# Strassen's algorithm for 10 of 44 block products in the last down projection of a two-layer encoder trunk

## The chip, the core and the metric

The kernel runs on one core of one Trainium2 chip. The metric is device time in microseconds (us). Three runs of the kernel before took 2696.85, 2698.23 and 2699.97 us; their median, 2698.23 us, is the time that counts.

## The reference

Two layers, each a token mixer (attention and a gating branch) and a gated convolutional FFN, and a last RMSNorm. The change touches the end of the second layer alone:

```python
def conv_ffn(h, w_up, conv_w, conv_b, w_down):
    ...
    return (jax.nn.gelu(acc) * b) @ w_down      # (256 x 5632) @ (5632 x 2048)

def reference(...):
    for l in range(DEPTH):                      # DEPTH = 2
        ...
        x = x + conv_ffn(rmsnorm(x, g_ffn[l]), w_up[l], conv_w[l], conv_b[l], w_down[l])
    return rmsnorm(x, g_final)
```

All tensors are float32; there are 256 rows (tokens) and 2048 columns of output.

## The kernel before

Every large product is float32 made of three products of the type float32r. `split_w` turns a tile of weights into two: ScalarE (ACT) copies it rounded, `hi` (line 109), and VectorE (DVE) subtracts, `lo = raw - hi` (line 110). The left operand is split likewise, once, into the two planes of an `operand()` tile. A product is then left_hi x hi + left_hi x lo + left_lo x hi: three matmuls of 512 columns (lines 118 to 120), which add up in one PSUM bank.

The last down projection takes the 22 tiles `gT[m]` as left operands. Each holds two k-tiles (`j` = 0, 1; 128 rows of the sum each) of 256 tokens in two halves (`t` = 0, 1). The output goes in four stretches `n` of 512 columns, one after the other. Within a stretch `rows()` walks `m` from 0 to 21: `fetch` brings 512 KB of weights (a tile `raw` of 128 x 2 x 512, issued by SyncE's queue, SP), `split_w` splits it, and TensorE (PE) does 2 `j` x 2 `t` x 3 = 12 matmuls. So a stretch is 264 matmuls and the projection 1056.

Buffers tie the engines together. There are five `raw` tiles: a fetch waits until an old tile has been split. There are three `hi` and three `lo` tiles: a split waits until PE has done with the tiles of the split three back, so that ACT and DVE run at most two splits ahead of the one PE works on. PSUM has eight banks: three pairs, `acc`, and two single ones, `tp`.

At the end of a stretch DVE adds the two banks to the residual (line 601), ACT sums squares (603) and GpSimd (POOL) multiplies by the gain `g_final` (605). The last stretch holds back the second half of the tokens for the last four `m` (`late=4`), so that the first half is done 24 matmuls before the second. Then for each half: the sum of squares is completed (612), POOL raises it to -1/2 (613), DVE and ACT scale the four stretches (618, 621), and they are written out.

Before the projection, POOL still makes the last two `gT` tiles (line 574, a product, and line 172, their second plane), and PE transposes the residual into `xb` through the `tp` banks (line 591; DVE copies out, 592).

The order in each engine's queue is set by a scheduler when the program is built; each queue is worked off strictly in that order. The functions that the change touches:

Of the kernel before, what the change touches and what calls it, by code (L numbers as in the profile page):

```python
# [41 lines left out]
def trunk_kernel(ctx, tc, x, g_mix, w_in, b_forget, g_sgu, w_spatial, b_spatial,  # L42
# [54 lines left out]
    def fetch(w2d, k0, nk, c0, cols):  # L97
        raw = wraw.tile([P, nk, cols], F32, tag="raw", name=nm("raw"))
        nc.sync.dma_start(raw, w2d[k0 * P:(k0 + nk) * P, c0:c0 + cols].rearrange("(k p) c -> p k c", p=P))
        return raw  # L100

    def split_w(raw, more=False, behind=None):
        shape = list(raw.shape)
# [5 lines left out]
        a = nc.scalar.copy(hi, raw)  # L109
        v = nc.vector.tensor_tensor(lo, raw, hi.bitcast(F32), op=ALU.subtract)  # L110
# [12 lines left out]
    def rows(w2d, c0, cols, ops, late=0):  # L123


        n = len(ops)
# [16 lines left out]
        return acc
# [443 lines left out]
    for m in range(KT // 2):
        tp = tp_bank()
        for k in range(2):
            for t in range(NT):  # L590
                nc.tensor.transpose(tp[:, (2 * t + k) * P:(2 * t + k + 1) * P], xT[m][:, k, t * P:(t + 1) * P], ident)
        nc.vector.tensor_copy(xb[m // 2][:, :, m % 2 * T:m % 2 * T + T], tp.rearrange("p (t c) -> p t c", t=NT))
    ss = small.tile([P, NT, NB], F32, tag="ss", name=nm("ss"))
    fin = small.tile([P, NT], F32, tag="fin", name=nm("fin"))
    for n in range(NB):
        gf = scratch([P, 512])
        nc.gpsimd.dma_start(gf, g_final[None, n * 512:(n + 1) * 512].broadcast_to([P, 512]))
        acc = rows(w_down[DEPTH - 1], n * 512, 512, gT, late=4 if n == NB - 1 else 0)
        for t in range(NT):
            z = xb[n][:, t, :]  # L600
            nc.vector.tensor_tensor(z, acc[t], z, op=ALU.add)
            junk = scratch([P, 512])
            nc.scalar.activation(junk, z, AF.Square, accum_out=ss[:, t, n:n + 1])
            if n < NB - 1:
                nc.gpsimd.tensor_tensor(z, z, gf, op=ALU.mult)
        if n == NB - 2:
            nc.vector.tensor_reduce(fin, ss[:, :, 0:NB - 1], axis=AX.X, op=ALU.add)
            nc.vector.tensor_scalar(fin, fin, 1.0 / D, EPS, op0=ALU.mult, op1=ALU.add)
    for t in range(NT):
        f_ = fin[:, t:t + 1]  # L610
        z = xb[NB - 1][:, t, :]
        nc.vector.scalar_tensor_tensor(f_, ss[:, t, NB - 1:NB], 1.0 / D, f_, op0=ALU.mult, op1=ALU.add)
        nc.gpsimd.tensor_tensor(f_, f_, mhalf[:, 0:1], op=ALU.pow)
        nc.vector.tensor_tensor(z, z, gf, op=ALU.mult)
        for n in range(NB):
            z = xb[n][:, t, :]
            if n % 2 == 0:
                nc.vector.tensor_scalar_mul(z, z, f_)
                nc.sync.dma_start(out_v[:, t, n * 512:(n + 1) * 512], z)
            else:  # L620
                nc.scalar.activation(z, z, AF.Identity, scale=f_)
# [30 lines left out]
```

## Time and profile before

| | |
|---|---|
| runs | 2696.85, 2698.23, 2699.97 us |
| profiled execution | 2697.62 us, of which span 2695.9 us |
| PE busy | 2681.0 us (99%) |
| DVE, ACT, POOL busy | 1608.7, 1268.8, 449.7 us |
| last projection | first matmul at 2444.74, last at 2686.59 us of the span |

A row of a timeline gives the start and the length in us, the engine, the line and operation, the tiles (out<-in), shapes, a count, and in brackets how long the engine idled before and what ended it. A PE row lasts longer than the step from one matmul to the next, because matmuls overlap in the array.

### The profile page before, as it was taken

Reading aid. Unit: us, or ns where it says so; the run is one execution under the profiler, and the core shown is the slowest. Engines: PE = TensorE matmul, PEld = TensorE weight load, DVE = VectorE, ACT = ScalarE, POOL = GpSimd, SP = SyncE. Lnnn points to the kernel's source line nnn. Section 1 sums busy time; section 2 is a strip of 40 time slices with the busy share of each in tenths; the row PEclk is TensorE's granted clock in tenths of the full one; section 3 lists DMA queues with packets and bytes.
Section 4 is the critical chain, followed back from the end, with each engine's and each line's share of the span. In section 5 each row is a group of like instructions: output and inputs, shape, how many; then the busy total and the mean of one; then the engine's idle time right before and its main releaser. Section 6 shows DMA issues by size and latency. Waiting matters only on the chain.

```text
span 2695.9 us, 36616 instructions
## 1 busy us (share of the span) xinstructions
PE 2681.0 (99%) x14384; PEld 2312.7 (86%) x14384; DVE 1608.7 (60%) x1728; ACT 1268.8 (47%) x1512; POOL 449.7 (17%) x381
## 2 busy tenths in 40 slices
PE   9999999999999999999999999999999999999998
PEld 7988888888888888888889888888888888888887
DVE  6555555566666676545555555555667676766444
ACT  5454554444444444444444545544544444444443
POOL 2201101112222222200002011011122222221000
PEclk9999999999999999999999999999999999999999
DMA  7566666656666666665665666666666666666664
GB/s 235 161 202 192 189 181 185 189 188 184 182 198 181 196 182 196 205 190 188 189 186 157 201 194 186 182 188 187 191 181 189 190 190 188 188 189 193 196 197 156
DMA packets 269557, 508.19 MB, mean 189 GB/s; under 512 B 16776, under 2 KB 33608, under 8 KB 269384
## 3 DMA queue, kind: packets, MB, share of 16 engines
q1 hardware_dynamic: 267144, 500.59, 61.5%
q0 software_dynamic: 1664, 4.21, 1.0%
q8 instruction: 112, 1.84, 0.3%
q10 hardware_dynamic: 576, 1.05, 0.1%
q14 instruction: 61, 0.50, 0.1%
HBM read 503.68 MB, written 2.11 MB: 188 GB/s over the span
## 4 chain that ended last, share of the span: by engine, by line
PE 97%; POOL 1%; issue 0%; ACT 0%; DMA 0%; DVE 0%; SPq 0%; POOLq 0%; ACTq 0%
PE acc L159 41%; PE acc L162 21%; PE acc L119 10%; PE acc L118 10%; PE acc L120 10%; PE tp L120 1%; PE tp L119 1%; PE tp L118 1%; POOL u L172 0%; POOL sq L190 0%; PE tp L522 0%; PE tp L467 0%; PE tp L484 0%; DMA u<-in_x_dram 0%; POOL tmp L418 0%
## 5 line engine op out<-in xcount | busy, mean ns | idle before, releaser
L110 DVE TENSOR_TENSOR lo<-raw,hi 128x1024 fp32r<-128x1024 f32 (+2 forms) x959 | 1221.9, 1278 | 1026.6 <-ACT hi L109 1025.5
L109 ACT CAST hi<-raw 128x1024 fp32r<-128x1024 f32 (+2 forms) x959 | 992.6, 1036 | 1223.9 <-PE acc L159 755.3
L159 PE MATMUL acc<-u,hi 128*128 128x512 f32 x4800 | 1485.7, 395 | 0.0
L162 PEld LDWEIGHTS acc<-u,lo 128*128 128x128 f32 x4800 | 883.2, 188 | 197.8 <-issue 0.9
L162 PE MATMUL acc<-u,lo 128*128 128x256 f32 x4800 | 927.7, 279 | 0.0
L159 PEld LDWEIGHTS acc<-u,hi 128*128 128x128 f32 x4800 | 744.6, 189 | 13.1
L119 PE MATMUL acc<-lo,u 128*128 128x512 f32 (+1 forms) x1352 | 521.1, 385 | 0.9 <-DVE lo L110 0.9
L118 PE MATMUL acc<-hi,u 128*128 128x512 f32 (+1 forms) x1352 | 517.6, 383 | 0.0
L120 PE MATMUL acc<-hi,u 128*128 128x512 f32 (+1 forms) x1352 | 515.3, 381 | 0.0
L119 PEld LDWEIGHTS acc<-lo,u 128*128 128x128 f32 x1352 | 254.8, 188 | 45.1 <-DVE lo L110 1.5
L118 PEld LDWEIGHTS acc<-hi,u 128*128 128x128 f32 x1352 | 254.7, 188 | 44.8
L120 PEld LDWEIGHTS acc<-hi,u 128*128 128x128 f32 x1352 | 254.6, 188 | 44.4
L558 POOL TENSOR_TENSOR tmp<-tmp,bc 128x512 f32<-128x512 f32 x44 | 58.3, 1325 | 373.5 <-DVE tmp L168 349.1
L565 DVE SCALAR_TENSOR_TENSOR tmp<-tmp,cv,tmp 128x256 f32<-128x256 f32 x176 | 117.5, 716 | 0.0
L190 POOL TENSOR_TENSOR sq<-sq,tmp 128x512 f32<-128x512 f32 x28 | 40.5, 1448 | 414.3 <-ACT tmp L189 413.2
L568 POOL TENSOR_TENSOR tmp<-tmp,bc 128x512 f32<-128x512 f32 x44 | 77.2, 1755 | 118.1 <-ACT tmp L567 118.1
L172 POOL TENSOR_TENSOR u<-tmp,u 128x512 fp32r<-128x512 f32 x52 | 88.2, 1701 | 32.4 <-ACT u L171 32.4
L574 POOL TENSOR_TENSOR tmp<-tmp,tmp 128x512 f32<-128x512 f32 x44 | 57.0, 1296 | 187.6 <-PE acc L162 152.1
L516 POOL TENSOR_TENSOR u<-u,tmp 128x512 f32<-128x512 f32 x16 | 28.3, 1789 | 319.0 <-DVE tmp L515 319.0
L167 ACT COPY tmp<-acc 128x512 f32<-128x512 f32 x112 | 65.2, 582 | 32.9 <-PE acc L162 32.9
L168 DVE TENSOR_TENSOR tmp<-acc,tmp 128x512 f32<-128x512 f32 x112 | 76.7, 685 | 1.2 <-ACT tmp L167 1.1
L567 ACT ACTIVATE tmp<-tmp 128x512 f32<-128x512 f32 x44 | 27.8, 631 | 53.4 <-DVE tmp L565 53.3
(159 smaller groups left out, 857.9 us busy)
## 6 DMA issues: line engine op xcount, KB each, us to landing
raw<-in_w_up_dram SPq DMA_DIRECT2D x352, 512.0 KB, 4.4
raw<-in_w_in_dram SPq DMA_DIRECT2D x255, 512.0 KB, 3.9
raw<-in_w_down_dram SPq DMA_DIRECT2D x176, 512.0 KB, 4.7
raw<-in_w_out_dram SPq DMA_DIRECT2D x64, 512.0 KB, 4.4
raw<-in_w_in_dram SPq DMA_DIRECT2D x48, 344.0 KB, 3.1
raw<-in_w_branch_b_dram SPq DMA_DIRECT2D x32, 512.0 KB, 4.5
raw<-in_w_branch_a_dram SPq DMA_DIRECT2D x32, 512.0 KB, 4.0
u<-in_x_dram SPq DMA_DIRECT2D x8, 256.0 KB, 7.0
```

Of the source, the lines that this page charges most:

```text
L109: a = nc.scalar.copy(hi, raw)
L110: v = nc.vector.tensor_tensor(lo, raw, hi.bitcast(F32), op=ALU.subtract)
L118: m0 = nc.tensor.matmul(o, lhsT=op[:, j, 0, ts], rhs=hi[:, jw, :], start=start, stop=False)
L119: nc.tensor.matmul(o, lhsT=op[:, j, 0, ts], rhs=lo[:, jw, :], start=False, stop=False)
L120: nc.tensor.matmul(o, lhsT=op[:, j, 1, ts], rhs=hi[:, jw, :], start=False, stop=stop)
L159: nc.tensor.matmul(acc[i][:, f, :], lhsT=hi[:, j, fs[f]], rhs=xhl, start=k == 0, stop=False, skip_group_check=True)
L162: nc.tensor.matmul(acc[i][:, f, 0:T], lhsT=lo[:, j, fs[f]], rhs=xh, start=False, stop=k == nk - 1, skip_group_check=True)
L167: nc.scalar.copy(dst, a[:, :, 1, :])
L168: nc.vector.tensor_tensor(dst, a[:, :, 0, :], dst, op=ALU.add)
L172: eng.tensor_tensor(op[:, :, 1, :], src, op[:, :, 0, :].bitcast(F32), op=ALU.subtract)
L565: nc.vector.scalar_tensor_tensor(y[:, f, :], a[:, f, tap:tap + T], cv[:, tap, ft:ft + 1], y[:, f, :], op0=ALU.mult, op1=ALU.add)
L568: nc.gpsimd.tensor_tensor(y, y, inv_b, op=ALU.mult)
```

## The change

The four stretches become two halves `g` of two stretches each (`q` = 0, 1), and each step `i` of a half brings two `raw` tiles, `ra` and `rb`, 1024 columns. For 17 of the 22 `m` nothing else changes: 24 matmuls ("a plain pair"). For five `m` (`AT`: steps 3, 7, 11, 15, 18 of half 0 and 1, 5, 9, 13, 17 of half 1) the 2 x 2 blocks of tokens and k-tiles times the 2 x 2 blocks of k-tiles and columns are multiplied by Strassen's algorithm in Winograd's form: seven products instead of eight, 21 matmuls. Each product or running sum has a bank of its own, eight in all: P1, P2, R3, Q4, R5, R6, R7, E.

The sums of weight blocks are done by DVE in float32, partly in place, and the four resulting sets are split. We call the splits of such a pair a (`ra`; products P1, P2), b (`rb` after line 680; R7, R3), c (`ra` after 684 and 685; R6, Q4) and d (`t1`, half size; R5). The sums of left blocks, `sums(m)`, are made once by POOL (one add over 512 columns, four subtracts of 128), copied by ACT (609), completed by DVE (610), and used by both halves. After the last such step of a half the banks P1, R5, R6, R7 are folded into the residual (lines 698 to 708). The last steps hold back two `m` instead of four.

```diff
+        nc.gpsimd.tensor_tensor(z, gT[m][:, :, 0, :].bitcast(F32), gT[m][:, :, 1, :].bitcast(F32), op=ALU.add)
+        nc.gpsimd.tensor_tensor(s_[:, 0, :], z[:, 0, P:T], z[:, 1, P:T], op=ALU.subtract)
...
+        nc.scalar.copy(hi, s_)
+        nc.vector.tensor_tensor(lo, s_, hi.bitcast(F32), op=ALU.subtract)
...
+    AT = ((3, 7, 11, 15, 18), (1, 5, 9, 13, 17))
+    LATE = 2
...
-    for n in range(NB):
-        acc = rows(w_down[DEPTH - 1], n * 512, 512, gT, late=4 if n == NB - 1 else 0)
+    for g in range(NB // 2):
+        b0, b1, b2, t0, t1_ = acc_banks(), acc_banks(), acc_banks(), tp_bank(), tp_bank()
+        bank = {"P2": b0[:, 0], "R3": b0[:, 1], "R6": b2[:, 0], "P1": b2[:, 1]}
+        bank.update({"Q4": b1[:, 0], "E": b1[:, 1], "R7": t0, "R5": t1_} if g == 0 else
+                    {"R7": b1[:, 0], "R5": b1[:, 1], "Q4": t0, "E": t1_})
...
+            nc.vector.tensor_tensor(t1, ra[:, 0, :], rb[:, 0, :], op=ALU.add)
+            nc.vector.tensor_tensor(rb[:, 0, :], rb[:, 0, :], rb[:, 1, :], op=ALU.add)
+            hi, lo = split_w(ra)
+            go("P1", A[0, 0], hi[:, 0, :], lo[:, 0, :], i == lastS)
+            go("P2", A[0, 1], hi[:, 1, :], lo[:, 1, :])
+            nc.vector.tensor_tensor(ra[:, 0, :], ra[:, 0, :], rb[:, 0, :], op=ALU.add)
+            nc.vector.tensor_tensor(ra[:, 1, :], ra[:, 1, :], ra[:, 0, :], op=ALU.add)
+            hi, lo = split_w(rb)
+            go("R7", s_[3], hi[:, 0, :], lo[:, 0, :], i == lastS)
+            go("R3", s_[4], hi[:, 1, :], lo[:, 1, :])
+            hi, lo = split_w(ra)
...
+            if i == lastS:
+                p1, v, z_ = scratch([P, 512]), scratch([P, 512]), scratch([P, 512])
+                nc.scalar.copy(p1, bank["P1"])
+                nc.vector.tensor_tensor(v, bank["R6"], p1, op=ALU.subtract)
...
+                nc.gpsimd.tensor_tensor(x[0, 0], x[0, 0], p1, op=ALU.add)
...
+                nc.gpsimd.tensor_tensor(x[1, 1], x[1, 1], z_, op=ALU.add)
```

Three places of the queues are of use below. First, POOL's queue at the start of the projection, before (`tmp` tiles are scratch, `u_20816` and `u_20823` the last two `gT`):

```order
L597 DMA tmp_20880<-in_g_final_dram 128x512
L574 TENSOR_TENSOR tmp_20812<-tmp_20812,tmp_20611 128x512
L574 TENSOR_TENSOR tmp_20819<-tmp_20819,tmp_20625 128x512
L172 TENSOR_TENSOR u_20816<-tmp_20812,u_20816 128x2x256
L172 TENSOR_TENSOR u_20823<-tmp_20819,u_20823 128x2x256
```

The same stretch of POOL's queue after:

```order
L604 TENSOR_TENSOR tmp_21007<-u_17241 128x512
L574 TENSOR_TENSOR tmp_20812<-tmp_20812,tmp_20611 128x512
L574 TENSOR_TENSOR tmp_20819<-tmp_20819,tmp_20625 128x512
L605 TENSOR_TENSOR tmp_21008<-tmp_21007 128x128
L607 TENSOR_TENSOR tmp_21008<-tmp_21007 128x128
L172 TENSOR_TENSOR u_20816<-tmp_20812,u_20816 128x2x256
L606 TENSOR_TENSOR tmp_21008<-tmp_21007,tmp_21008 128x128
L172 TENSOR_TENSOR u_20823<-tmp_20819,u_20823 128x2x256
L604 TENSOR_TENSOR tmp_21170<-u_18037 128x512
L608 TENSOR_TENSOR tmp_21008<-tmp_21007,tmp_21008 128x128
L605 TENSOR_TENSOR tmp_21171<-tmp_21170 128x128
```

The sums of left blocks for the first Strassen pairs are woven into the work that was there; those of the third, fourth and fifth pair follow at once. DVE's queue in the first Strassen pair, after (`lo_21032` is split b, `lo_21042` c, `lo_21052` d, `lo_21063` the next plain split; L594 copies a transposed tile out of a `tp` bank):

```order
L684 TENSOR_TENSOR raw_21003<-raw_21003,raw_21005 128x512
L685 TENSOR_TENSOR raw_21003<-raw_21003 128x512
L110 TENSOR_TENSOR lo_21032<-raw_21005,hi_21031 128x1024
L594 COPY u_20828<-tp_20854 128x2x256
L594 COPY u_20828<-tp_20860 128x2x256
L110 TENSOR_TENSOR lo_21042<-raw_21003,hi_21041 128x1024
L594 COPY u_20829<-tp_20866 128x2x256
L695 TENSOR_TENSOR lo_21052<-tmp_21016,hi_21051 128x512
L594 COPY u_20829<-tp_20872 128x2x256
L610 TENSOR_TENSOR u_20878<-tmp_21008,u_20878 128x512
L610 TENSOR_TENSOR u_20879<-tmp_21171,u_20879 128x512
L110 TENSOR_TENSOR lo_21063<-raw_21058,hi_21062 128x1024
```

The copies that free the `tp` banks stand between the splits; banks R7 and R5 of half 0 are these `tp` banks. Second, DVE's queue where one stretch ended and the next began, before:

```order
L110 TENSOR_TENSOR lo_22128<-raw_22125,hi_22127 128x1024
L601 TENSOR_TENSOR u_20828<-acc_21696,u_20828 128x512 x2
L110 TENSOR_TENSOR lo_22146<-raw_22143,hi_22145 128x1024
L607 TENSOR_REDUCE fin_20879<-ss_20878 128x2
L608 TENSOR_SCALAR fin_20879<-fin_20879 128x2
L110 TENSOR_TENSOR lo_22164<-raw_22161,hi_22163 128x1024
```

After, at the seam of the two halves (`lo_21830` is the last split of half 1's plain step 0, `lo_21865` split a and `lo_21877` split b of its Strassen step 1):

```order
L110 TENSOR_TENSOR lo_21830<-raw_21823,hi_21829 128x1024
L716 TENSOR_TENSOR u_20826<-acc_20890,u_20826 128x512
L716 TENSOR_TENSOR u_20827<-acc_20890,u_20827 128x512
L716 TENSOR_TENSOR u_20826<-acc_20891,u_20826 128x512
L716 TENSOR_TENSOR u_20827<-acc_20891,u_20827 128x512
L110 TENSOR_TENSOR lo_21865<-raw_21857,hi_21864 128x1024
L679 TENSOR_TENSOR tmp_21861<-raw_21857,raw_21859 128x512
L722 TENSOR_REDUCE fin_20885<-ss_20884 128x2
L680 TENSOR_TENSOR raw_21859<-raw_21859 128x512
L723 TENSOR_SCALAR fin_20885<-fin_20885 128x2
L684 TENSOR_TENSOR raw_21857<-raw_21857,raw_21859 128x512
L685 TENSOR_TENSOR raw_21857<-raw_21857 128x512
```

Four evictions stand where two stood, and a Strassen pair's sums right behind them. Third, the end of DVE's queue, before:

```order
L601 TENSOR_TENSOR u_20829<-tp_22105,u_20829 128x512
L612 SCALAR_TENSOR_TENSOR fin_20879<-ss_20878,fin_20879 128x1
L614 TENSOR_TENSOR u_20829<-u_20829,tmp_22103 128x512
L618 TENSOR_SCALAR u_20826<-u_20826,fin_20879 128x512
L618 TENSOR_SCALAR u_20828<-u_20828,fin_20879 128x512
L601 TENSOR_TENSOR u_20829<-tp_22106,u_20829 128x512
L612 SCALAR_TENSOR_TENSOR fin_20879<-ss_20878,fin_20879 128x1
```

And after (`tp_21819` is bank Q4, `tp_21820` bank E, which PE fills last):

```order
L716 TENSOR_TENSOR u_20828<-tp_21819,u_20828 128x512
L727 SCALAR_TENSOR_TENSOR fin_20885<-ss_20884,fin_20885 128x1
L731 TENSOR_TENSOR u_20828<-u_20828,tmp_21812 128x512
L727 SCALAR_TENSOR_TENSOR fin_20885<-ss_20884,fin_20885 128x1
L731 TENSOR_TENSOR u_20829<-u_20829,tmp_21813 128x512
L727 SCALAR_TENSOR_TENSOR fin_20885<-ss_20884,fin_20885 128x1
L731 TENSOR_TENSOR u_20828<-u_20828,tmp_21812 128x512
L735 TENSOR_SCALAR u_20826<-u_20826,fin_20885 128x512
L735 TENSOR_SCALAR u_20828<-u_20828,fin_20885 128x512
L716 TENSOR_TENSOR u_20829<-tp_21820,u_20829 128x512
L727 SCALAR_TENSOR_TENSOR fin_20885<-ss_20884,fin_20885 128x1
```

Between the eviction of Q4 and that of E now stand eight operations of DVE, where four stood between the last two evictions before. PE's order keeps `hi` before `lo` in a plain step: two matmuls with the new `hi`, then one with the new `lo`.

More of the change, by code (lines that the diff above doesn't have):

```diff
@@ new lines, in trunk_kernel, with three @@
+    NG = FT // 2
+    AT = ((3, 7, 11, 15, 18), (1, 5, 9, 13, 17))
+    LATE = 2
+    S = []
+    for i in range(len(AT[0])):
+        if i < 4:
+            u_ = unit([2, 4, P], F32R)
+            hi, lo = u_[:, 0], u_[:, 1]
+        else:
+            hi, lo = (xpool.tile([P, 4, P], F32R, tag=f"x{2 * (i - 4) + q}", name=nm("sx")) for q in range(2))
+        S.append((hi, lo))
+    Sx = {}
+    def three(bank, started, A, hi, lo, last):
+        for q, (l_, r_) in enumerate(((A[0], hi), (A[0], lo), (A[1], hi))):
+            nc.tensor.matmul(bank, lhsT=l_, rhs=r_, start=q == 0 and not started, stop=last and q == 2)
@@ L593, in trunk_kernel, with go, plain @@
     ss = small.tile([P, NT, NB], F32, tag="ss", name=nm("ss"))
     fin = small.tile([P, NT], F32, tag="fin", name=nm("fin"))
-    for n in range(NB):
-        gf = scratch([P, 512])
-        nc.gpsimd.dma_start(gf, g_final[None, n * 512:(n + 1) * 512].broadcast_to([P, 512]))
-        acc = rows(w_down[DEPTH - 1], n * 512, 512, gT, late=4 if n == NB - 1 else 0)
-        for t in range(NT):
[L600 to L607, printed above, removed]
+    for g in range(NB // 2):
+        n0 = 2 * g
+        gf = [scratch([P, 512]) for _ in range(2)]
+        for q in range(2):
+            nc.gpsimd.dma_start(gf[q], g_final[None, (n0 + q) * 512:(n0 + q + 1) * 512].broadcast_to([P, 512]))
+        b0, b1, b2, t0, t1_ = acc_banks(), acc_banks(), acc_banks(), tp_bank(), tp_bank()
+        bank = {"P2": b0[:, 0], "R3": b0[:, 1], "R6": b2[:, 0], "P1": b2[:, 1]}
+        bank.update({"Q4": b1[:, 0], "E": b1[:, 1], "R7": t0, "R5": t1_} if g == 0 else
+                    {"R7": b1[:, 0], "R5": b1[:, 1], "Q4": t0, "E": t1_})
+        seen = set()
+        order = list(range(NG))
+        paired = dict(zip(AT[g], AT[0]))
+        if g == 1:
+            rest = [m for m in range(NG) if m not in AT[0]]
+            order = []
+            for i in range(NG):
+                order.append(paired[i] if i in paired else rest.pop(0))
+        w2d = w_down[DEPTH - 1]
+        held = []
+        def go(name, A, hi, lo, last=False):
+            three(bank[name], name in seen, A, hi, lo, last)
+            seen.add(name)
+        out_of = {(0, 0): "P2", (0, 1): "R3", (1, 0): "Q4", (1, 1): "E"}
+        def plain(A, ws, t, last):
+            for q in range(2):
+                for j in range(2):
+                    go(out_of[t, q], A[t, j], ws[q][0][:, j, :], ws[q][1][:, j, :], last and j == 1)
+        lastS = max(paired)
+        for i, m in enumerate(order):
+            A = left(m)
+            ra, rb = (fetch(w2d, 2 * m, 2, (n0 + q) * 512, 512) for q in range(2))
+            if i not in paired:
+                late = g == 1 and NG - i <= LATE
+                ws = [split_w(r_, more=late and i < NG - 1) for r_ in (ra, rb)]
+                if late:
+                    held.append((A, ws, i == NG - 1))
+                for t in range(1 if late else NT):
+                    plain(A, ws, t, i == NG - 1)
+                continue
+            if m not in Sx:
+                Sx[m] = sums(m, *S[AT[0].index(m)])
+            s_ = Sx[m]
+            t1 = scratch([P, 512])
+            nc.vector.tensor_tensor(t1, ra[:, 0, :], rb[:, 0, :], op=ALU.add)
[9 more added lines that the diff above has]
+            hi, lo = split_w(ra)
+            go("R6", s_[2], hi[:, 0, :], lo[:, 0, :], i == lastS)
+            go("Q4", A[1, 1], hi[:, 1, :], lo[:, 1, :])
+            hi = wspl.tile([P, 512], F32R, tag="hi", name=nm("hi"))
+            lo = wspl.tile([P, 512], F32R, tag="lo", name=nm("lo"))
+            nc.scalar.copy(hi, t1)
+            nc.vector.tensor_tensor(lo, t1, hi.bitcast(F32), op=ALU.subtract)
+            go("R5", s_[1], hi, lo, i == lastS)
+            if i == lastS:
+                p1, v, z_ = scratch([P, 512]), scratch([P, 512]), scratch([P, 512])
+                nc.scalar.copy(p1, bank["P1"])
+                nc.vector.tensor_tensor(v, bank["R6"], p1, op=ALU.subtract)
+                nc.vector.tensor_tensor(z_, bank["R7"], v, op=ALU.add)
+                x = {(t, q): xb[n0 + q][:, t, :] for t in range(NT) for q in range(2)}
+                nc.gpsimd.tensor_tensor(x[0, 0], x[0, 0], p1, op=ALU.add)
+                nc.vector.tensor_tensor(x[0, 1], bank["R5"], x[0, 1], op=ALU.add)
+                nc.vector.tensor_tensor(x[1, 1], bank["R5"], x[1, 1], op=ALU.add)
+                nc.gpsimd.tensor_tensor(x[0, 1], x[0, 1], v, op=ALU.add)
+                nc.gpsimd.tensor_tensor(x[1, 0], x[1, 0], z_, op=ALU.subtract)
+                nc.gpsimd.tensor_tensor(x[1, 1], x[1, 1], z_, op=ALU.add)
+        for q in range(2):
+            for A, ws, last in held:
+                for j in range(2):
+                    go(out_of[1, q], A[1, j], ws[q][0][:, j, :], ws[q][1][:, j, :], last and j == 1)
+        for t in range(NT):
+            for q in range(2):
+                z = x[t, q]
+                nc.vector.tensor_tensor(z, bank[out_of[t, q]], z, op=ALU.add)
+                junk = scratch([P, 512])
+                nc.scalar.activation(junk, z, AF.Square, accum_out=ss[:, t, n0 + q:n0 + q + 1])
+                if g == 0:
+                    nc.gpsimd.tensor_tensor(z, z, gf[q], op=ALU.mult)
+        if g == 0:
+            nc.vector.tensor_reduce(fin, ss[:, :, 0:2], axis=AX.X, op=ALU.add)
```

17 lines of the change are left out of this document (14 added, 3 removed).

## The prediction

> **What bounds the kernel now.** I read the page's busy times and its chain first, then a window of the last projection.
>
> ```profile
> PE 2681.0 (99%) x14384; PEld 2312.7 (86%) x14384; DVE 1608.7 (60%) x1728; ACT 1268.8 (47%) x1512; POOL 449.7 (17%) x381
> PE 97%; POOL 1%; issue 0%; ACT 0%; DMA 0%; DVE 0%; SPq 0%; POOLq 0%; ACTq 0%
> 2500.00:2560.00 60.00, 60.00 (x266) 49.70 (x266) 28.99 (x24) 24.60 (x27) 3.59 (x3) 1.00 0.64 198
> ```
>
> PE is the bound, in the whole and in this stage; the window's columns after the length are PE, PE's weight loads, DVE, ACT, POOL, clock, DMA share, GB/s. So a matmul taken away is time won, if everything that feeds PE keeps its lead. The timeline shows that lead:
>
> ```profile
> 2512.52 0.39 PE L120 MATMUL acc<-hi,u 128*128 128x512 f32 x1
> 2512.74 0.39 PE L118 MATMUL acc<-hi,u 128*128 128x512 f32 x1
> 2512.99 1.05 ACT L109 CAST hi<-raw 128x1024 fp32r<-128x1024 f32 x1 [1.67 <-PE acc L120]
> 2514.07 1.22 DVE L110 TENSOR_TENSOR lo<-raw,hi 128x1024 fp32r<-128x1024 f32 x1 [0.66 <-ACT hi L109]
> 2515.24 0.39 PE L120 MATMUL acc<-hi,u 128*128 128x512 f32 x1
> ```
>
> Twelve matmuls start in 2515.24 - 2512.52 = 2.72 us, 0.227 us each. When a split's last matmul is through, ACT refills its buffer 0.25 us after the next split's first matmul; `lo` ends at 2515.29, 2.55 us after that matmul. PE has two more splits ready, 5.44 us, so 2.9 us are spare.
>
> **What DVE and POOL do to each other.** Duration alone doesn't tell what the added sums cost:
>
> ```profile
> 2508.71 1.22 DVE L110 TENSOR_TENSOR lo<-raw,hi 128x1024 fp32r<-128x1024 f32 x1
> 2509.27 3.06 POOL L605 TENSOR_TENSOR u<-u,tmp 128x512 f32<-128x512 f32 x2 [54.77 <-ACT tmp L603]
> 2511.35 2.06 DVE L110 TENSOR_TENSOR lo<-raw,hi 128x1024 fp32r<-128x1024 f32 x1 [1.43 <-ACT hi L109]
> 2628.95 3.05 POOL L605 TENSOR_TENSOR u<-u,tmp 128x512 f32<-128x512 f32 x2 [56.26 <-ACT tmp L603]
> 2629.71 1.07 DVE L608 TENSOR_SCALAR fin<-fin 128x2 f32<-128x2 f32 x1
> 2449.38 4.59 POOL L172 TENSOR_TENSOR u<-tmp,u 128x512 fp32r<-128x512 f32 x2
> 2450.42 1.27 DVE L592 COPY u<-tp 128x512 f32<-128x512 f32 x2
> ```
>
> A DVE split that starts inside a POOL operation ends 1.08 us after it (2511.35 + 2.06 = 2513.41, POOL's end 2512.33): it stood still and then ran its 1.22, less 0.14 of overlap. Even a 128x2 operation took 1.07. The split at 2508.71, which was first, lost nothing, and POOL's two took 3.06. Copies out of PSUM beside POOL ran at 0.64 each, undisturbed. So POOL's and DVE's operations on SBUF exclude each other, first come first served. The Trainium skill, "SBUF — State Buffer", section "Who interferes with whom", states this as an exclusive lock for the whole instruction, taken by a tensor_tensor with both inputs in SBUF against GpSimd's reads, and not by one with an input in PSUM; by that rule the sum is the one below, and were they independent it would be that of the second rival. The trace agrees (2.06 against 1.22). Durations for what is added:
>
> ```profile
> L574 POOL TENSOR_TENSOR tmp<-tmp,tmp 128x512 f32<-128x512 f32 x44 | 57.0, 1296 | 187.6 <-PE acc L162 152.1 <-DVE tmp L168 35.5
> L198 POOL TENSOR_TENSOR sq<-sq 128x256 f32<-128x256 f32 x4 | 4.0, 998 | 0.3
> L614 DVE TENSOR_TENSOR u<-u,tmp 128x512 f32<-128x512 f32 x2 | 1.4, 688 | 0.0
> L601 DVE TENSOR_TENSOR u<-acc,u 128x512 f32<-128x512 f32 x6 | 3.9, 686 | 1.2 <-PE acc L120 1.2
> L171 ACT CAST u<-tmp 128x512 fp32r<-128x512 f32 x52 | 32.0, 619 | 8.3 <-POOL tmp L418 5.4 <-POOL tmp L574 0.9
> raw<-in_w_down_dram SPq DMA_DIRECT2D x82, 512.0 KB, 4.7
> 2466.91 0.87 PE tp L591 x8
> 2444.74 0.40 PE L118 MATMUL acc<-hi,u 128*128 128x512 f32 x1
> 2445.79 1.59 DVE L110 TENSOR_TENSOR lo<-raw,hi 128x1024 fp32r<-128x1024 f32 x1 [0.93 <-ACT hi L109]
> ```
>
> POOL's 128-column subtract isn't in the trace: between a quarter of L574 (0.32) and half of L198 (0.50); I take 0.46, nearer the row of smaller size, since a fixed part doesn't shrink. On SBUF a POOL operation then blocks DVE for its length less 0.14: 1.15 and 0.32.
>
> **The sum, term by term.**
>
> *Matmuls gone:* 10 pairs x 3 x 0.227 = -6.8 us. SP still issues the same 88 fetches of 512 KB; ACT gets 10 casts for split d and 5 for the sums (0.62 each, 25 of 60 us busy): no cost.
>
> *Eight steady pairs.* DVE does 4 x 0.69 + 3 x 1.22 + 0.69 = 7.1 us in such a pair against PE's 21 x 0.227 = 4.8; with three plain pairs 14.4 against 21.1. On average it fits, so what counts is the lead. Splits a, b, c feed six matmuls each (1.36 us), d three. The next plain split takes b's buffer: from b's last matmul it needs 0.25 + 1.05 + 0.03 + 1.22 + 0.05 = 2.6 us to its `lo`; PE has nine matmuls of c and d and two with the new `hi`: 2.5. It waits 0.1, and about as much once more before the lead is back: 8 x 0.15 = +1.2. Ends: 0, and 0.5 a pair (4) where a late sum or fetch adds to it.
>
> *The first pair* (half 0, step 3). PE would reach its fifth batch of transposes in this stage 19.4 us after the stage's first matmul (72 + 6 matmuls, 16 transposes at 0.11). They need a `tp` bank that DVE's copy frees, and that copy stands behind split b. From 1.05 us on (the row at 2445.79) DVE has six splits and four sums on SBUF before it, 10.1 us. POOL, which has its two products, two second planes and the sums for the coming pairs, gets between them six operations of 512 columns and some eight small ones: 6 x 1.15 + 8 x 0.32 = 9.5. Together 20.7, the copy 0.6: PE waits 1.7. Behind it bank R5 waits for the last copy, after c and d (0.8), and the third matmul of R7 for the sums' second plane (0.4). Now b is released late, near the pair's end: the next plain `hi` comes 0.9 after PE is free, and its `lo`, behind another POOL operation, 1.3 later. Sum +5.2. Ends: 1.7 (only the last two, without POOL) and 6.5 (small operations of 0.6).
>
> *The seam* (half 1, step 1). Count from half 0's last matmul. DVE's four evictions end at 2.6. POOL's four gain multiplies ask from 2.2 on, each as soon as a square is summed, and one gets in ahead of each of DVE's next long operations: split a ends at 4.6, the first sum at 6.3, the sum for b at 8.1, the 128x2 step at 9.3, the two sums for c at 10.7. PE has a plain pair (5.4) and a (1.4), so it wants b's `hi` at 6.8 and gets it at 9.2; two matmuls on it wants c's at 9.7 and gets it at 11.8; the second plain `hi`, needed early in PE's order, costs 0.4. +5.0. Ends: 1.2 without POOL, 6. Before, a stretch's end had two evictions, each followed by plain splits with 2.9 us spare.
>
> *The two folds.* After each half's last Strassen step DVE has the difference and the two evictions of R5 (2.1 us) between the first and the second plain split, which would be done 0.5 us late, and one POOL add in front of it: 2 x 1.0 = +2.0; ends 1 and 3.
>
> *The end.*
>
> ```profile
> 2686.59 0.39 PE L120 MATMUL tp<-hi,u 128*128 128x512 f32 x1
> 2687.02 0.69 DVE L601 TENSOR_TENSOR u<-tp,u 128x512 f32<-128x512 f32 x1 [1.84 <-PE tp L120]
> 2687.75 0.63 ACT L603 ACTIVATE tmp<-u 128x512 f32<-128x512 f32 x1 [2.11 <-DVE u L601]
> 2688.50 0.16 DVE L612 SCALAR_TENSOR_TENSOR fin<-ss,fin 128x1 f32<-128x1 f32 x1 [0.79 <-ACT tmp L603]
> 2688.74 0.94 POOL L613 TENSOR_TENSOR fin<-fin,mhalf 128x1 f32<-128x1 f32 x1 [4.47 <-DVE fin L612]
> 2689.72 1.33 ACT L621 ACTIVATE u<-u,fin 128x512 f32<-128x512 f32 x2 [1.25 <-POOL fin L613]
> 2684.30 0.88 DVE L618 TENSOR_SCALAR u<-u,fin 128x512 f32<-128x512 f32 x2 [0.47 <-POOL fin L613]
> ```
>
> The last eviction now starts 0.43 us after the last matmul starts, and all else follows. After the change Q4 ends twelve matmuls earlier, so its eviction starts at -2.72 + 0.43 = -2.29, and between it and E's stand three operations of 0.16, three of 0.69 and two of 0.44: with itself 4.1 us. E's eviction starts at 1.8 instead of 0.43. The chain behind it is the same: +1.4; ends 1.2 and 2.2 (POOL's power blocking DVE).
>
> Sum: -6.8 + 1.2 + 5.2 + 5.0 + 2.0 + 1.4 = +8.0 us. The profiled execution took 2697.62 us, 0.6 under the median of the runs shown; on the median that gives 2706.2.
>
> **Rivals.**
>
> *The lead covers all.* If the waits at the first pair, the seam, the folds and the steady pairs don't come, because splits run further ahead than I step them, the matmuls' 6.8 us come in but for the end's 1.4: 2692.8. About 0.2%, 5.4 us, is what a measurement here tells from no change, so this ends faster only if all added waits, the end's with them, stay under 1.4. For it: DVE idles half of the window. Against it: the lead is two splits, and at the three places DVE owes more than that.
>
> *POOL falls into DVE's gaps.* Without exclusion the first pair costs 2.5, the seam 1.2, the folds 1.1, with 1.2 and 1.4 as above: 7.4 - 6.8 = +0.6, 2698.8. For it: 94% of the window has no POOL work. Against it: POOL's work is set free by the very evictions and stage start that load DVE.
>
> *Fetches stop DVE.* The first sum of a pair, t1, needs the weights of both stretches and stands in DVE's queue ahead of a plain split. By the five buffers, b's fetch goes out when the split five before it is done, some 2.1 us before PE starts on that one; it lands at +2.6, t1 takes 0.7 and the plain split 1.2: 4.5, against 5.4 when PE wants it. Landings of 6.5 us would cost 1 us in each of ten pairs: 10 more than forecast, 2716. Against it:
>
> ```profile
> SPq L99 <- DVE lo L110: 183.2, 80, 3.2
> ```
>
> SP's queue waited 183 us for freed buffers in this stage; it isn't behind.
>
> That the change does not do what it says is excluded: PE's queue has 30 matmuls less.
>
> **How the numbers follow.** My forecast, exclusion at the three places: 0.64. POOL in the gaps: 0.22. Fetches: 0.09. The lead covers all: 0.05. Likeliest 2706.2; its own range, from half of the waits at the three places (12.2 / 2 = 6.1 less) to 5 us more, 2700 to 2711. The range reaches down past the second rival, to 2697.5, and up to 2712; outside lie the first rival and most of the fetches. Faster by over 0.2%: 0.05. Within 0.2% (2692.8 to 2703.6): 0.22 and, of the forecast's lower end, 0.08, together 0.30. Slower: 0.65.
>
> **What will show it.** Right: PE idles in the waits view on DVE `lo` and ACT `hi` at the first pair (about 20 to 29 us into the stage) and 7 to 13 us after half 1 begins, under 0.3 us in the pairs between; DVE splits of about 2 us there, beside POOL. The stage's matmuls span some 248 to 249 us, not 242, and the last matmul to the span's end 1.4 us more than now (9.3). Wrong: PE idle under 3 us in the stage, or DVE's splits at 1.22 beside POOL; or idle at every pair, released by a DMA.

## The result, and the profile after

The changed kernel takes 2710.62 us (median of 4 runs, 2708.36 to 2712.35), the one before 2698.20 (4 runs): ratio 1.0045, 95% interval 1.0033 to 1.0057. It is slower by more than the 0.2% that can be told apart. The forecast was 2706.2, its range 2697.5 to 2712.0. The profiled execution took 2711.51 us with a span of 2709.8, so 13.9 us more than the profiled one before. The page's busy times and the head of its chain:

```profile
PE 2683.8 (99%) x14354; PEld 2307.7 (85%) x14354; DVE 1670.6 (62%) x1805; ACT 1287.8 (48%) x1539; POOL 485.0 (18%) x412
PE 95%; DVE 2%; POOL 1%; DMA 1%; issue 1%; ACT 1%; SPq 0%; POOLq 0%; DVEq 0%; ACTq 0%
```

PE has its 30 matmuls less, and yet 2.8 us more busy time: some matmuls got longer. DVE, 0% of the chain before, is 2% now. The same 60 us of the last projection that the prediction showed for the kernel before:

```profile
2500.00:2560.00 60.00, 59.36 (x260) 48.05 (x259) 42.48 (x46) 30.31 (x32) 3.74 (x5) 1.00 0.62 194
```

DVE went from 29.0 to 42.5 us in it and PE stood idle for only 0.6: in the middle of a half the pairs cost little. So most of the loss is at a few places. The waits of the last projection (who waited for whom, total, times, longest):

```profile
DVE tmp L679 <- DMA raw<-in_w_down_dram: 27.4, 9, 4.8
...
PE acc L628 <- ACT hi L109: 4.7, 3, 3.4
PE acc L628 <- DVE lo L110: 4.0, 5, 1.4
...
PE tp L593 <- DVE u L594: 1.2, 1, 1.2
```

*The first pair.* PE's waits there come where the forecast had them: 1.3 us on the copy of a transposed tile, 0.5 on the one that frees bank R5, 0.8 on the next plain `hi`, 1.6 on its `lo`. Beside POOL, DVE's operations stretch (timeline; start, duration; in brackets the idle time before and its releaser):

```profile
2461.82 1.61 POOL L604 TENSOR_TENSOR tmp<-u 128x512 f32<-128x512 f32 x1
2462.33 1.66 DVE L685 TENSOR_TENSOR raw<-raw 128x512 f32<-128x512 f32 x1
2471.53 1.28 POOL L604 TENSOR_TENSOR tmp<-u 128x512 f32<-128x512 f32 x1
2471.76 3.54 DVE L110 TENSOR_TENSOR lo<-raw,hi 128x1024 fp32r<-128x1024 f32 x2 [1.03 <-ACT hi L109]
2473.95 0.50 PE L628 MATMUL acc<-lo,u 128*128 128x512 f32 x1 [1.44 <-DVE lo L110]
```

The weight sum for c takes 1.66 us where 0.69 is free, two splits 3.54 where 2.4 are, and PE stands behind them.

*The seam.* DVE, POOL, ACT and PE after half 0's last matmul:

```profile
2572.35 2.48 DVE L716 TENSOR_TENSOR u<-acc,u 128x512 f32<-128x512 f32 x4
2574.59 1.30 POOL L720 TENSOR_TENSOR u<-u,tmp 128x512 f32<-128x512 f32 x1 [10.17 <-ACT tmp L718]
2574.75 2.23 DVE L110 TENSOR_TENSOR lo<-raw,hi 128x1024 fp32r<-128x1024 f32 x1
2576.44 1.70 POOL L720 TENSOR_TENSOR u<-u,tmp 128x512 f32<-128x512 f32 x1
2576.90 1.78 DVE L679 TENSOR_TENSOR tmp<-raw,raw 128x512 f32<-128x512 f32 x1
2578.67 2.51 POOL L720 TENSOR_TENSOR u<-u,tmp 128x512 f32<-128x512 f32 x2
2578.71 3.02 DVE L680 TENSOR_TENSOR raw<-raw 128x512 f32<-128x512 f32 x1
2581.90 1.04 ACT L109 CAST hi<-raw 128x1024 fp32r<-128x1024 f32 x1 [5.54 <-DVE fin L723]
2583.00 0.73 PE L628 MATMUL acc<-hi,u 128*128 128x512 f32 x2 [3.40 <-ACT hi L109]
```

Split a and the two sums behind it take 2.23, 1.78 and 3.02 where 1.22, 0.69 and 0.69 are free: 4.4 us, which is the seam's wait. The sum for b waits out two gain multiplies in one go. (The cast at 2581.90 waits for that sum's end at 2581.73; the view names the 128x2 step that ended just after it.)

*What the forecast had no term for.* The windows view, cut where the granted clock changes (columns: length, PE, PEld, DVE, ACT, POOL, clock, DMA share, GB/s):

```profile
2471.05:2474.46 3.41, 1.30 (x5) 0.77 (x5) 2.70 (x2) 2.57 (x3) 3.26 (x4) 1.00 0.03 10
2474.46:2477.88 3.42, 3.42 (x9) 2.66 (x9) 2.23 (x2) 0.00 (x0) 3.00 (x3) 0.50 0.65 196
...
2580.28:2583.69 3.41, 0.69 (x2) 0.30 (x2) 3.38 (x5) 1.44 (x2) 0.90 (x1) 1.00 0.08 25
2583.69:2587.10 3.41, 2.75 (x7) 2.17 (x7) 2.46 (x3) 1.18 (x2) 0.00 (x0) 0.50 0.36 112
2587.10:2590.52 3.42, 3.42 (x9) 2.67 (x8) 1.23 (x1) 2.07 (x3) 0.00 (x0) 0.50 0.64 200
```

After each of the two places PE ran at half its clock, one stretch of 3.41 us and one of 6.83, with 9 matmuls in a full window where 15 fit. That is +4.5 us.

*A sum that waits for a transfer,* at the pairs at steps 9 and 17 of half 1:

```profile
2615.65 1.23 DVE L110 TENSOR_TENSOR lo<-raw,hi 128x1024 fp32r<-128x1024 f32 x1 [1.04 <-ACT hi L109]
2617.51 1.05 ACT L109 CAST hi<-raw 128x1024 fp32r<-128x1024 f32 x1 [1.89 <-PE tp L628]
2621.67 0.69 DVE L679 TENSOR_TENSOR tmp<-raw,raw 128x512 f32<-128x512 f32 x1 [4.79 <-DMA raw<-in_w_down_dram]
2624.27 0.50 PE L628 MATMUL acc<-lo,u 128*128 128x512 f32 x1 [1.14 <-DVE lo L110]
...
2665.23 0.69 DVE L679 TENSOR_TENSOR tmp<-raw,raw 128x512 f32<-128x512 f32 x1 [4.09 <-DMA raw<-in_w_down_dram]
2667.84 0.50 PE L628 MATMUL acc<-lo,u 128*128 128x512 f32 x1 [0.43 <-DVE lo L110]
```

The cast of the plain split before the pair at step 9 was done at 2618.56, but its `lo` stood behind `t1` in DVE's queue, and `t1` waited until 2621.67 for b's weights. PE lost 1.4 us around it, and 0.7 in the same way ahead of step 17.

*The end.* The last matmul starts at 2699.56:

```profile
2700.01 0.88 DVE L735 TENSOR_SCALAR u<-u,fin 128x512 f32<-128x512 f32 x2
2700.81 0.68 DVE L716 TENSOR_TENSOR u<-tp,u 128x512 f32<-128x512 f32 x1
```

Bank E's eviction starts 1.25 us after it (0.43 before), behind the scalings of the first 128 tokens.

The account of the two profiled executions, from the starts of successive matmuls (a matmul is worth 0.2267 us, a transpose 0.109, what is over is lost):

| term | forecast | measured |
|---|---|---|
| matmuls gone | -6.8 | -6.8 |
| first pair | +5.2 | +5.0 |
| seam | +5.0 | +4.5 |
| two folds | +2.0 | +0.9 (half 0's; half 1's cost nothing) |
| eight steady pairs | +1.2 | +4.7 (1.4 and 0.7 of it ahead of steps 9 and 17 of half 1) |
| the end | +1.4 | +0.9 |
| half clock behind first pair and seam | none | +4.5 (1.6 and 3.0) |
| before the stage | none | +0.2 |
| sum | +8.0 | +13.9 |

The two folds differ in DVE's queue:

```profile
2556.17 0.68 DVE L704 TENSOR_TENSOR u<-tp,u 128x512 f32<-128x512 f32 x1
2556.76 0.68 DVE L705 TENSOR_TENSOR u<-tp,u 128x512 f32<-128x512 f32 x1
2557.36 1.94 DVE L110 TENSOR_TENSOR lo<-raw,hi 128x1024 fp32r<-128x1024 f32 x1
...
2678.12 0.68 DVE L700 TENSOR_TENSOR tmp<-acc,tmp 128x512 f32<-128x512 f32 x1
2678.72 1.72 DVE L110 TENSOR_TENSOR lo<-raw,hi 128x1024 fp32r<-128x1024 f32 x1
2680.37 0.68 DVE L701 TENSOR_TENSOR tmp<-acc,tmp 128x512 f32<-128x512 f32 x1
```

In half 0 both evictions of R5 stand ahead of the second plain split, as the forecast had it; in half 1 only the first difference does, and PE doesn't wait there.

### The profile page after: what moved, and what is told of

Same layout as the page of the kernel before. It is cut to its first block, busy times and chain, and to the rows that moved or that the text cites. A ratio compares the mean times of both kernels' runs of the same rounds, so it can differ in the third digit from the quotient of the medians.

```text
span 2709.8 us, 36721 instructions
## 1 busy us (share of the span) xinstructions
PE 2683.8 (99%) x14354; PEld 2307.7 (85%) x14354; DVE 1670.6 (62%) x1805; ACT 1287.8 (48%) x1539; POOL 485.0 (18%) x412
## 4 chain that ended last, share of the span: by engine, by line
PE 95%; DVE 2%; POOL 1%; DMA 1%; issue 1%; ACT 1%; SPq 0%; POOLq 0%; DVEq 0%; ACTq 0%
PE acc L159 41%; PE acc L162 21%; PE acc L119 8%; PE acc L118 8%; PE acc L120 8%; PE acc L628 5%; PE tp L628 1%; DVE lo L110 1%; DMA raw<-in_w_down_dram 1%; ACT hi L109 0%; POOL u L172 0%; POOL sq L190 0%; PE tp L522 0%; PE tp L467 0%; PE tp L484 0%
## 5 line engine op out<-in xcount | busy, mean ns | idle before, releaser
L110 DVE TENSOR_TENSOR lo<-raw,hi 128x1024 fp32r<-128x1024 f32 (+2 forms) x969 | 1238.2, 1283 | 959.2 <-ACT hi L109 957.8
L119 PE MATMUL acc<-lo,u 128*128 128x512 f32 (+1 forms) x1088 | 417.5, 384 | 0.9 <-DVE lo L110 0.9
L118 PE MATMUL acc<-hi,u 128*128 128x512 f32 (+1 forms) x1088 | 414.1, 381 | 0.0
L120 PE MATMUL acc<-hi,u 128*128 128x512 f32 (+1 forms) x1088 | 411.8, 378 | 0.0
L119 PEld LDWEIGHTS acc<-lo,u 128*128 128x128 f32 x1088 | 204.8, 188 | 34.7 <-DVE lo L110 1.5
L628 PE MATMUL acc<-hi,u 128*128 128x512 f32 x498 | 164.8, 397 | 4.7 <-ACT hi L109 4.7
L628 PE MATMUL acc<-lo,u 128*128 128x512 f32 x249 | 100.0, 402 | 4.0 <-DVE lo L110 4.0
```

What stands on the lines that cost most here:

```text
L118: m0 = nc.tensor.matmul(o, lhsT=op[:, j, 0, ts], rhs=hi[:, jw, :], start=start, stop=False)
L119: nc.tensor.matmul(o, lhsT=op[:, j, 0, ts], rhs=lo[:, jw, :], start=False, stop=False)
L120: nc.tensor.matmul(o, lhsT=op[:, j, 1, ts], rhs=hi[:, jw, :], start=False, stop=stop)
L628: nc.tensor.matmul(bank, lhsT=l_, rhs=r_, start=q == 0 and not started, stop=last and q == 2)
```

## The experiments

The theory: the time is lost in the waits at the first pair and the seam, where POOL's operations on SBUF shut out a DVE that is already full, and in the half clock that these waits bring. The rivals: the two-half structure by itself; a first pair that costs the same wherever it stands; DVE's own queue without POOL; transfers; a half clock that has nothing to do with the waits. Each run is compared with runs of the kernel before on the same chip (medians 2698.07 to 2698.91). The intervals of four runs (half 0's first pair later, no sums of POOL, matmuls of zeros, the first weight sum moved) overlap that of the changed kernel, so what is read from these rests on their traces. Losses of PE are taken from the starts of its matmuls, as in the account.

**No Strassen pair at all.**

```diff
-    AT = ((3, 7, 11, 15, 18), (1, 5, 9, 13, 17))
+    AT = ((), ())
...
-        lastS = max(paired)
+        lastS = -1
+        x = {(t, q): xb[n0 + q][:, t, :] for t in range(NT) for q in range(2)}
```

> The two halves, the banks and the end as in the changed kernel, but no Strassen pair in either half: all 22 pairs of k-tiles plain, 1,056 matmuls in the stage as before the change, no sums, no folds. My theory (the lost time is in the waits at the first pair, at half 1's first pair and at the folds, and in TensorE's clock going to half after the first two of them): no wait over 0.5 us in the stage, no stretch at a granted clock of 0.5, stage 242 us from the first to the last matmul start as before, and the later end alone costs 0.9 to 1.6 us: 2699 to 2700. Rival, that the two-half structure with its gain multiplies on GpSimd and its eviction of four banks is itself what costs: the stage shows waits at the seam without any Strassen pair, 2702 or more.

2699.55 us, ratio 1.0005 (0.9997 to 1.0014). The waits view shows no wait of PE in the stage, the clock stays at 1.00, and the first to the last matmul start takes 241.9 us as before. The same 60 us, and the end:

```profile
2500.00:2560.00 60.00, 60.00 (x266) 49.72 (x265) 27.12 (x23) 23.20 (x22) 0.00 (x0) 1.00 0.62 194
```

```profile
2688.38 0.39 PE L628 MATMUL tp<-hi,u 128*128 128x512 f32 x1
2689.73 0.68 DVE L717 TENSOR_TENSOR u<-tp,u 128x512 f32<-128x512 f32 x1
```

The last eviction 1.35 us after the last matmul's start instead of 0.43 is the whole loss that the trace shows from the stage's first matmul on (0.9). The halves, their four gain multiplies included, cost nothing as long as no pair stands behind them.

**Half 0's first pair later.**

```diff
-    AT = ((3, 7, 11, 15, 18), ...
+    AT = ((6, 9, 12, 15, 18), ...
```

> Half 0's Strassen pairs at steps 6, 9, 12, 15, 18 instead of 3, 7, 11, 15, 18; nothing else moves. My theory (at step 3 VectorE still owes the splits and the copies of the transposes that the stage began with, and GpSimd's sums shut it out; the half clock follows from these waits): the first pair's 5.0 us of waits shrink to 1.4 to 1.9 and the 1.6 us at half clock behind them go, with two plain pairs instead of three between the others costing up to 0.5 more: 2704 to 2706. Rival, that a first pair waits for its own sums wherever it stands: the same 5 us of waits at step 6, 2710 to 2711. Rival, that three plain pairs between two are needed and two don't rebuild the lead: each pair of half 0 waits 1 us or more, 2708 to 2712.

2706.05 us, ratio 1.0025 (1.0016 to 1.0035), at the expectation's upper end. The 5.0 us of waits and the half clock behind them are gone; the pair loses 1.0 at step 6. So it isn't the pair but its place. The four later pairs of half 0, the fold included, lose 2.2, as the four later ones of the changed kernel did (2.2), so two plain pairs between two are enough and the second rival fails. The seam lost 6.6; ahead of steps 9 and 13 of half 1 1.4 and 0.6 were lost.

**Half 1's first pair later.**

```diff
-    AT = (..., (1, 5, 9, 13, 17))
+    AT = (..., (4, 8, 11, 14, 17))
```

> Half 1's Strassen pairs at steps 4, 8, 11, 14, 17 instead of 1, 5, 9, 13, 17; half 0 as in the changed kernel. My theory (at step 1 VectorE owes four evictions, and GpSimd's four gain multiplies get in ahead of its next operations): the 4.5 us of waits at half 1's first pair and the 3.0 us at half clock behind them go, 2703 to 2704. Rival, that the loss at the seam is the pair's own (its sums for c stand too close to its splits) and would follow the pair to step 4: no gain there, 2710 to 2711. Rival, that the half clock has nothing to do with the waits: the waits go and a stretch at half clock stays near the seam, 2706.

2702.30 us, ratio 1.0013 (1.0005 to 1.0022), 0.7 under the expectation's lower end. From the 132nd to the 146th microsecond of the stage nothing is lost (7.5 before) and the clock stays full; the first pair loses its 4.9 and 1.5 as in the changed kernel. Half 1's pairs lose 1.6 in all, where those behind the seam lost 3.3 in the changed kernel; that is more than the 0.7 by which the time is lower than expected.

**Without POOL's sums.**

```diff
-        z, s_ = scratch([P, 2, T]), scratch([P, 4, P])
-        nc.gpsimd.tensor_tensor(z, gT[m][:, :, 0, :].bitcast(F32), gT[m][:, :, 1, :].bitcast(F32), op=ALU.add)
...
-        nc.scalar.copy(hi, s_)
+        z = gT[m][:, :, 0, :].bitcast(F32)
+        nc.scalar.copy(hi.rearrange("p (j a) c -> p j (a c)", j=2), z)
...
```

> Leaves out the sums of activations for the Strassen products: ScalarE's cast and VectorE's subtraction take the activations themselves, so 25 GpSimd operations of half 0 (5 of 512 columns and 20 of 128) are gone, and the result of these products is not the reference's. All splits, weight sums, matmuls and casts are there. My theory (GpSimd's operations on SBUF shut VectorE out in the first 25 us of the stage): the first pair's 5.0 us of waits fall to 1.5 to 2.5, no half clock behind them, the steady pairs of half 0 keep 0.3 less, half 1 as it was: 2705 to 2706. Rival, that VectorE's own queue there (six splits, four sums, then the copies of transposes) makes the waits by itself: 4 us or more of them stay, 2709 to 2711.

2707.16 us, ratio 1.0030 (1.0019 to 1.0042). The first pair's waits fall from 5.0 to 2.0 and no half clock follows. DVE's three splits there run at 1.2 each:

```profile
2469.38 3.49 DVE L110 TENSOR_TENSOR lo<-raw,hi 128x1024 fp32r<-128x1024 f32 x3
```

So 3 of the 5 us are POOL's, 2 are DVE's own queue. The total is 1.2 over the expectation's upper end: the pair at step 9 of half 1, which waits for a transfer, lost 2.0 here instead of 1.4, and the other pairs of half 0 0.7 more.

**Without POOL's gain multiplies.**

```diff
-                if g == 0:
-                    nc.gpsimd.tensor_tensor(z, z, gf[q], op=ALU.mult)
```

> Leaves out GpSimd's four multiplies by the last gain in half 0, so the first 1,024 columns of the output lack that gain; all else as in the changed kernel. My theory (at the seam these four multiplies on SBUF get in ahead of VectorE's next operations): the 4.5 us of waits there fall to 1 to 1.5, and with them the 3.0 us at half clock go, 2704 to 2705. Rival, that VectorE's four evictions and its own queue make the seam's waits: 3 us or more of them stay, and the half clock with them, 2708 to 2710.

2703.30 us, ratio 1.0018 (1.0009 to 1.0027), 0.7 under the expectation's lower end. The same operations of DVE at the seam:

```profile
2571.89 2.48 DVE L716 TENSOR_TENSOR u<-acc,u 128x512 f32<-128x512 f32 x4
2574.29 1.22 DVE L110 TENSOR_TENSOR lo<-raw,hi 128x1024 fp32r<-128x1024 f32 x1
2575.42 0.69 DVE L679 TENSOR_TENSOR tmp<-raw,raw 128x512 f32<-128x512 f32 x1
...
2576.14 0.69 DVE L680 TENSOR_TENSOR raw<-raw 128x512 f32<-128x512 f32 x1
```

1.22, 0.69, 0.69: the sum for b ends 4.94 us after the first eviction's start, 9.38 in the changed kernel. The seam loses 0.7 instead of 4.5, and the clock stays full. So all but 0.7 of the seam's waits come from POOL's gain multiplies. In this execution the half clock behind the first pair was missing too, although that pair still lost 4.9 in waits; the edit doesn't touch it.

**Filling the seam's waits with matmuls of zeros.**

```diff
+            if g == 1 and i == 1:
+                for _ in range(14):
+                    nc.tensor.matmul(bank["P2"], lhsT=zero, rhs=..., start=False, stop=False)
             go("R7", s_[3], hi[:, 0, :], lo[:, 0, :], i == lastS)
...
+                for _ in range(3):
...
```

> At half 1's first pair TensorE gets 14 matmuls of zeros, added to a bank that holds other sums, ahead of the first matmul that waited 3.56 us there, and 3 more ahead of the next that waited; they fit into the waits. All else as in the changed kernel. My theory (the clock goes to half behind the seam because TensorE stands idle there): TensorE is busy through the waits, no stretch at half clock behind the seam, 3.0 us less, 2707 to 2708.5. Rival, that the half clock comes from something else than TensorE's own idle time: the stretch of 6.8 us at 0.5 stays, 2710 to 2711.

2708.36 us, ratio 1.0036 (1.0023 to 1.0048). The window of the wait, and the one behind it:

```profile
2580.00:2583.41 3.41, 3.24 (x14) 2.05 (x12) 3.38 (x5) 1.39 (x2) 0.95 (x1) 1.00 0.09 25
2583.41:2586.82 3.41, 2.75 (x12) 2.17 (x12) 2.51 (x3) 2.18 (x3) 0.00 (x0) 1.00 0.46 117
```

DVE and ACT are as late as ever, PE is busy, and the clock stays at 1.00. The seam cost 5.4 us instead of 7.5 (3.9 of it the added matmuls). In the four profiled executions with this wait left open (the changed kernel, half 0's first pair later, no sums of POOL, the first weight sum moved) the half clock followed it each time. So it comes from PE's standing idle. The run's whole gain isn't all the edit's: in the profiled execution the half clock behind the first pair, which the edit doesn't touch, was missing too (1.6), and ahead of steps 9 and 17 of half 1 1.4 less was lost.

**The first weight sum behind the split before it.**

```diff
-            nc.vector.tensor_tensor(t1, ra[:, 0, :], rb[:, 0, :], op=ALU.add)
+            behind_ = last_lo[0]
+            after(nc.vector.tensor_tensor(t1, ra[:, 0, :], rb[:, 0, :], op=ALU.add), behind_)
```

> The first weight sum of each pair is kept behind the split of the plain stretch before it in VectorE's queue; nothing else moves. My theory (this sum waits for a transfer while a finished cast stands behind it): the wait of 1.4 us at the pair at step 9 of half 1 goes and the smaller ones at other pairs get shorter, 1 to 2.5 us in all: 2708 to 2709.5; the first pair and the seam lose what they lost. Rival, that the fetch itself is late, so that the sum, moved back or not, holds up the pair's own splits: no gain, 2710 to 2711.

2708.05 us, ratio 1.0035 (1.0022 to 1.0047). The 27.4 us in which DVE's first sum waited for transfers are gone from the view, and nothing is lost ahead of steps 9 and 17 of half 1 (1.4 and 0.7 before). So what these waits cost PE in the changed kernel is those 2.1 us. The first pair lost its 5.0 in waits again, but with no half clock behind them. The windows of this execution show why:

```profile
2470.04:2473.45 3.41, 2.47 (x10) 1.27 (x8) 2.37 (x3) 2.09 (x3) 3.33 (x4) 1.00 0.33 112
2473.45:2476.87 3.42, 2.23 (x10) 1.86 (x11) 3.42 (x3) 0.85 (x1) 3.34 (x4) 1.00 0.28 84
2476.87:2480.28 3.41, 3.41 (x17) 2.83 (x16) 1.74 (x2) 1.38 (x2) 1.29 (x2) 1.00 0.72 238
```

The same waits fell into two windows, each with PE busy for 2.2 us or more, not 1.30 in one.

**Both first pairs later.** The two edits of `AT` together.

> Both halves' first pairs later: half 0 at steps 6, 9, 12, 15, 18 and half 1 at 4, 8, 11, 14, 17. My theory (the losses at the two places are independent, and each half clock belongs to its waits): the gains of the two single moves add, 4.6 and 8.3 us off the changed kernel's 2710.6, so 2697 to 2698.5, no stretch at half clock in the stage, and what is left against the 6.8 us saved is 5 to 6 us of small waits at pairs and folds and 0.9 at the end. Rival, that the saved waits turn into others at the pairs that now stand closer together: 2700 or more.

2697.52 us, ratio 0.9996 (0.9987 to 1.0005): no difference from the kernel before that can be told apart. The two gains add (2710.6 - 4.6 - 8.3 = 2697.7). The stage takes 239.2 us against 241.9 before, 4.2 of the 6.8 saved are lost in small waits, and the end costs 1.0.

**Pins at the sums and the end.** The edit of the first weight sum above, and

```diff
-                nc.vector.tensor_scalar_mul(z, z, f_)
+                scaled = nc.vector.tensor_scalar_mul(z, z, f_)
+                if t == 0:
+                    after(scaled, evict)
...
```

> Both halves' first pairs later (6, 9, 12, 15, 18 and 4, 8, 11, 14, 17), each pair's first weight sum behind the plain split before it in VectorE's queue, and at the end the scalings of the first 128 rows behind the last eviction. My theory: of the 4.2 us of waits left in the stage with the pairs later, the 1 to 2 that come from sums waiting for transfers go, and the last matmul to the span's end falls from 10.3 to 9.4: 2694.5 to 2696.5. Rival, that the waits left are VectorE's work at the pairs and not its queue: only the end's 0.8 comes, 2696.5 to 2697.

2695.74 us, ratio 0.9990 (0.9981 to 0.9998). The number lies in the expected range, the theory's first half doesn't hold: DVE's waits for transfers fell from 21.9 to 0.2 us and the stage stayed at 239.2. With the pairs later, those waits were in DVE's spare time; what is left are DVE's own operations in the pairs. Only the end gained, from 10.3 to 9.7 us between the last matmul's start and the span's end, 0.6 and not 0.9: the last square now waits 0.3 for ACT's scalings of the first 128 tokens.

**The folds behind a split.**

```diff
+                if i == lastS + 1:
+                    for f in folds:
+                        after(f, last_lo[0])
...
```

> As the one before, and the four VectorE operations of each fold behind the second split of the plain stretch that follows the last pair. My theory (a fold's operations stand between two splits that TensorE is about to want): the 0.8 us of wait behind half 0's last pair goes, and up to 0.3 at half 1's: 0.5 to 1.1 less than the one before, 2693.5 to 2696. Rival, that GpSimd's adds of the fold shut VectorE out of the next splits wherever the fold stands: no gain.

2695.17 us, ratio 0.9987 (0.9978 to 0.9996). All waits of PE for more than its own sequence in this stage:

```profile
PE acc L631 <- DVE lo L112: 0.8, 3, 0.3
```

The stage is 238.7 us, 0.5 shorter than with the folds where they were: half 0's fold costs 0.5 now instead of 0.9. The two medians' intervals overlap, so that this last step is faster rests on the trace.

**Six pairs in each half.** `AT = ((5, 8, 11, 14, 16, 18), (4, 7, 10, 13, 15, 18))`.

> As the one before with six pairs in each half, at steps 5, 8, 11, 14, 16, 18 and 4, 7, 10, 13, 15, 18: six matmuls fewer, -1.4 us, at the price of one plain pair between some of them. If a lead of two splits is rebuilt in one plain pair, 1 us less than the one before, 2692.5 to 2695. Rival (three splits and four sums of VectorE in a pair, 7.1 us against TensorE's 4.8, are not made up in one plain pair of 5.4 us against 2.4): 0.5 to 1 us of wait at each of the close pairs takes the gain back or more, 2694 to 2698.

2696.95 us, ratio 0.9994 (0.9985 to 1.0002). Six matmuls less, and 2.3 us more lost in the stage. The pairs at step 16 of half 0 and 15 of half 1, with one plain pair before them, lose 0.9 and 0.5, which is the rival's price; but the pair at step 18, with one before it too, loses no more than it did, and 0.8 more is lost at steps 5 and 11 of half 0. So one plain pair between two doesn't always rebuild the lead. Its end went back to 10.3 us: the first of the last evictions starts 2.7 us ahead of the last matmul's start, not 3.4, and the last one, behind the gain multiplies in DVE's queue, 1.1 after it, not 0.5. The kernel with pins and folds stays the fastest.

## Why the prediction was right, and where it wasn't

*Right: slower, and at the places named.* What a pair costs depends on where it stands. By the forecast's terms the first pair was 5.2 (5.0 measured), the seam 5.0 (4.5), the end 1.4 (0.9). That POOL and DVE exclude each other on SBUF carried the first two: without POOL's sums the first pair lost 2.0, between the 1.7 and the 2.5 that the prediction gave without POOL and without exclusion, and without the gain multiplies the seam lost 0.7 against its 1.2. POOL's subtract of 128 columns, taken as 0.46 us, took 0.45 to 0.46 alone.

*The first pair, in detail.* 1.7, 0.8, 0.4, 0.9, 1.3 were the waits stepped; 1.3, 0.5, under 0.3, 0.8, 1.6 came.

*The seam, in detail.* The order was right but for one place: POOL's last two multiplies went ahead of the sum for b together, not one of them ahead of the 128x2 step. b's `hi` came 3.6 late, not 2.4, and c's 0.8, not 2.1.

*What failed: the step from waits to time.* The sum counts each wait of PE as its own length. At the first pair and the seam it cost half as much again, 4.5 us on 9.5, because the clock fell behind it. So the stage's matmuls span 254.6 us, not the 248 to 249 forecast. That 4.5 is also about the distance between the forecast and the median (2710.6 - 2706.2 = 4.4) is luck: the other differences, +3.5 at the steady pairs, -2.3 at the first pair, the seam, the folds and the end, and +0.2 before the stage, add 1.4, and the median lies 0.9 below the profiled execution, while the one before lies 0.6 above its own. That the range held is in part luck too: its upper end, 2712.0, was worked out from waits alone, and one of the four runs (2712.35) lies above it.

*Steady pairs: mis-sized.* 0.15 each was stepped from the splits alone, and a pair with nothing else in its way came near it: 0.20 to 0.25 in every run with pairs. The measured 4.7 for eight is above the upper end given (4). Of it, 2.1 come by the mechanism that the third rival had: the sum `t1` waits for b's fetch in front of a plain split. It waited at 9 of the 10 pairs, 27.4 us in all, and cost PE something worth naming at two. The rival had the wait right and its price wrong: DVE had that time to spare at the others. So the sign "under 0.3 us in the pairs between" held for most of them, not for all.

*The folds: mis-stepped.* Both were taken to stand alike in DVE's queue. Half 0's cost 0.9, about the 1.0 forecast, half 1's nothing.

*The first rival* (all waits hidden) ended nowhere near. *The second* (POOL in DVE's gaps) is out by the two runs without POOL's work.

## What to carry to other kernels

Work that fits on average can still cost more than it saves if it starts where the feeding engines already owe something: look for the stage's start and for evictions, and place it two or three steps behind them. When a sum of waits on TensorE is made, add what the clock does after them: here a window of 3.41 us in which TensorE was busy less than half cost another 1.6 to 3 us. A long wait on an engine that isn't the bound costs nothing while that engine has time to spare: with the pairs later 22 us of it went away and the stage stayed as long, and in the changed kernel 2.1 of 27.4 us reached TensorE.
